# A split-float weight tile on TensorE: the upper part meets both parts of x in one 512-column product

## The chip, the cores and the metric

One core of a Trainium2 chip (trn2) runs the whole program. The metric is the device time of one execution in microseconds; the kernel before was run three times: median 2190.94 us (2187.36 to 2192.04).

## The reference, cut to what matters

Two layers. Each is a token mixer (grouped attention and pooling) followed by a product-key expert mixer; 256 tokens, width 1024, everything in float32. The change is in the expert mixer:

```python
q = (xblk @ w_query).reshape(B, TOKEN_BLOCK, N_PEER_HEADS, 2, SUBKEY_DIM)
s = jnp.einsum('bthpd,hpnd->bthpn', q, sub_keys)
...
u = expert_u[eidx]
h = jnp.einsum('btd,bthkd->bthk', xblk, u)
act = jax.nn.gelu(h, approximate=False) * g
return jnp.einsum('bthk,bthkd->btd', act, expert_v[eidx])
```

The kernel does not gather: it multiplies x with all 16384 rows of `expert_u`, applies Gelu, multiplies by a gate that is zero for every expert a token did not choose, and multiplies with all of `expert_v`.

## The kernel before, in words

**Split operands.** Float32 products are made of three products of the float32r type. Each operand is split in an upper part (`wh`, `xh`: a rounding copy on ACT) and a lower part (`wl`, `xl`: the rest, a subtraction on DVE), and wh·xh + wh·xl + wl·xh is summed in one bank of PSUM. `weights` (L78 to L84) loads a 128x1024 tile by DMA on SP's queue (512 KB, four buffers `raw`), and `split` (L70 to L76) makes `wh` on ACT (L74) and `wl` on DVE (L75), two buffers each.

**A transposed product.** `transposed_product` (L98) takes one weight tile as eight 128x128 blocks and x as eight chunks of 128 rows by 256 tokens. `mm3` (L86 to L96) issues 24 products of 256 columns into half a bank: first 16 with the eight upper blocks, each block twice (against `xh`, then `xl`), and then eight with the lower blocks against `xh`. Every product loads its own stationary block.

**Stages of the expert mixer** (`peer`, L543), once per layer, here called by letters:
- Q: `queries` (L582): 32 tiles of `w_query`, two per bank of tag `mm`, copied out by one ACT instruction (L591); `key_scores` (L593) multiplies a head's queries with its keys; DVE finds the 16 best of each (`top16`, L536).
- U0 and U1: 64 tiles of `expert_u` each (L706 to L720), two tiles per bank of tag `mm`, evicted by one ACT Gelu of 512 columns per pair (L718). Beside U0 runs `routing` on DVE (L622); beside U1 runs `gating` (L676) on DVE and TensorE, for the half of the experts that U0 made.
- V: 128 tiles of `expert_v` (L724 to L741), each 12 products of 512 columns (L738) into four banks of tag `y`; gating of the second half runs beside its first 64 tiles.

**What sets the order.** `Pace` (L234) hands out steps of the side work by rate: `work(1.25)` per tile in U0, `work(1.05)` in U1; `side` hands out the dot products of the modulation (`ada_dot`, L142: one 512 KB load and one DVE instruction of 1024 columns each), 0.3 per tile in U1 of layer 0, none in U of layer 1. The framework places the instructions of each engine in one in-order queue when the program is built; the order in a queue can differ from the order in the text. PSUM has eight banks: two of tag `mm`, two of tag `g` and four of tag `y`; `y` is free in Q and U but for some short products that keep TensorE busy (`keep_warm`, L179).

Of the kernel before, what the change touches and what calls it, by code (L numbers as in the profile page):

```python
# [9 lines left out]
F32 = mybir.dt.float32  # L10
F32R = mybir.dt.float32r
# [3 lines left out]
AF = mybir.ActivationFunctionType  # L15
ALU = mybir.AluOpType
AX = mybir.AxisListType

P = 128
S = 256  # L20
# [29 lines left out]
def encoder_kernel(ctx, tc, x, c, ada_w, small, qkw, w_in1, w_in2, w_attn_o, mix_w, w_pool_o, w_out,  # L50
# [13 lines left out]
    def bank(tag):  # L64
        return psum.tile([P, 512], F32, name=tag, tag=tag, bufs=4 if tag == "y" else 2)
# [12 lines left out]
    def weights(src, shape):  # L78
        raw = rawtile()
        nc.sync.dma_start(raw, src)  # L80
        view = raw if len(shape) == 2 else raw.rearrange("p (a b) -> p a b", b=shape[2])
        if len(shape) == 4:
            view = raw.rearrange("p (a b c) -> p a b c", b=shape[2], c=shape[3])
        return split(view, shape)  # L84

    def mm3(acc, ws, xs, order="wx"):  # L86

        n = len(ws)
        if order == "wx":
            todo = [(k, 0, p) for k in range(n) for p in range(2)] + [(k, 1, 0) for k in range(n)]  # L90
        elif order == "x":
            todo = [(k, w, 0) for k in range(n) for w in range(2)] + [(k, 0, 1) for k in range(n)]
        else:
            todo = [(k, w, p) for k in range(n) for w, p in ((0, 0), (1, 0), (0, 1))]
        for m, (k, w, p) in enumerate(todo):
            PE.matmul(acc, ws[k][w], xs[k][p], start=m == 0, stop=m == 3 * n - 1)  # L96

    def transposed_product(src, xs, acc, order="wx"):  # L98

        wt = weights(src, [P, 8, P])  # L100
        mm3(acc, [(wt[0][:, dc], wt[1][:, dc]) for dc in range(8)],
            [(xs[0][:, dc], xs[1][:, dc]) for dc in range(8)], order)

    zeros = const.tile([P, 512], F16, name="zeros")
    V.memset(zeros, 0.0)
# [113 lines left out]
            return acc  # L219

    def xpair():
        return (xsp.tile([P, 8, S], F32R, name="xh", tag="xh"), xsp.tile([P, 8, S], F32R, name="xl", tag="xl"))

    def modulated(l, which, norm, xs, r, chunks):
        shift = lambda dc: mods[:, l, 24 * which + dc:24 * which + dc + 1]
        xn = lambda dc: norm.space[:, S * dc:S * dc + S]
        for dc in chunks:
            V.scalar_tensor_tensor(xn(dc), xT[:, dc], scaled[:, l, which, dc:dc + 1], r, op0=ALU.mult, op1=ALU.mult)
            A.activation(xs[0][:, dc], xn(dc), AF.Identity, bias=shift(dc))
        for dc in chunks:  # L230
            V.scalar_tensor_tensor(xs[1][:, dc], xn(dc), shift(dc), xs[0][:, dc].bitcast(F32),  # L231
                                   op0=ALU.add, op1=ALU.subtract)

    class Pace:  # L234
# [19 lines left out]
    def mixer(l, arena, parts, norm, side):  # L254
# [5 lines left out]
        probs = [f(52 + 2 * i, 54 + 2 * i).rearrange("p (a s) -> p a s", s=S) for i in range(2)]  # L260
        pTs = [f(56 + 2 * i, 58 + 2 * i).rearrange("p (a s) -> p a s", s=S) for i in range(2)]
        scr = [f(60 + 2 * i, 62 + 2 * i) for i in range(2)]
        pf = lambda a, b: parts[:, a * 256:b * 256].rearrange("p (c t) -> p c t", t=S)
        o = (pf(0, 8), pf(8, 16))
        mixed = (pf(16, 20), pf(20, 24))
        merged = (pf(24, 32), pf(32, 40))

        xs = xpair()

        def column_step(accs, cg, dp):  # L270
            wt = weights(w_in1[l, cg, dp], [P, 2, 512])
            late = l > 0 and cg == 2
            for w, p in ((0, 0), (1, 0), (0, 1)) if late else ((0, 0), (0, 1), (1, 0)):
                for tt in range(NT):
                    for d in range(2):
                        PE.matmul(accs[tt], xs[p][:, 2 * dp + d, tt * P:tt * P + P], wt[w][:, d],  # L276
                                  start=dp + d + w + p == 0, stop=dp == 3 and d == 1 and (p if late else w) == 1)

        def column_end(accs, cg):
# [155 lines left out]
        def values(h):  # L435
            ov = bank("y")[:, :S]
            for sc in range(2):
                v0 = 1280 + h // (NH // NKV) * DH
                PE.matmul(ov, proj[:, sc, v0:v0 + DH], pTs[h % 2][:, sc], start=sc == 0, stop=sc == 1)  # L439
            A.activation(o[0][:, h], ov, AF.Copy)  # L440
            V.tensor_tensor(o[1][:, h], ov, o[0][:, h].bitcast(F32), ALU.subtract)

        def attend(step):
            side(0.9)
# [39 lines left out]
        for g2 in range(2):  # L484
            acc = bank("mm").rearrange("p (a t) -> p a t", t=S)
            for k in range(2):
                g = 2 * g2 + k
                PE.matmul(acc[:, k], mw[:, g * P:g * P + P], mT[:, g], start=True, stop=True)
            for k in range(2):
                g = 2 * g2 + k  # L490
                ps = pscale[:, l, g:g + 1]
                A.activation(mixed[0][:, g], acc[:, k], AF.Copy, scale=ps)
                V.scalar_tensor_tensor(mixed[1][:, g], acc[:, k], ps, mixed[0][:, g].bitcast(F32),
                                       op0=ALU.mult, op1=ALU.subtract)
            if g2 == 0:
                attend(9)
# [4 lines left out]
        for c2 in range(4):  # L501
            pacc = bank("y").rearrange("p (a t) -> p a t", t=S)
            wt = weights(w_pool_o[l, c2], [P, 2, 4, P])
            for k in range(2):
                mm3(pacc[:, k], [(wt[0][:, k, g], wt[1][:, k, g]) for g in range(4)],
                    [(mixed[0][:, g], mixed[1][:, g]) for g in range(4)])
            for k in range(2):
                ct = 2 * c2 + k
                aacc = bank("mm")[:, :S]
                transposed_product(w_attn_o[l, ct], o, aacc)  # L510
                side(0.5)
                ga, gp = gates[:, ct], gates[:, 8 + ct]
                V.tensor_tensor(gp, pacc[:, k], gp, ALU.mult)
                V.tensor_tensor(ga, aacc, ga, ALU.mult)
                V.tensor_tensor(ga, ga, gp, ALU.add)
                A.activation(merged[0][:, ct], ga, AF.Copy)
                V.tensor_tensor(merged[1][:, ct], ga, merged[0][:, ct].bitcast(F32), ALU.subtract)

        norm = Norm(arena[:, 48 * 256:], lean=True)
        for c2 in range(4):  # L520
# [22 lines left out]
    def peer(l, arena, norm, side):  # L543
# [35 lines left out]
        work = Pace()  # L579
        qTs, kts = {}, {}  # L580

        def queries(h, c2):  # L582
            if c2 == 0:
                kts[h] = f(60 + 2 * (h % 2), 62 + 2 * (h % 2))
                nc.sync.dma_start(kts[h], keys[l, h])
                qTs[h] = f(4 * (h % 2), 4 * (h % 2) + 4).rearrange("p (c t) -> p c t", t=S)
            acc = bank("mm").rearrange("p (a t) -> p a t", t=S)
            for k in range(2):
                transposed_product(w_query[l, 4 * h + 2 * c2 + k], xs, acc[:, k], "x" if h + c2 + k == 0 else "wx")
                work(1)  # L590
            A.activation(qTs[h][:, 2 * c2:2 * c2 + 2], acc, AF.Copy)  # L591

        def key_scores(h):  # L593
            sacc = bank("g").rearrange("p (t q n) -> p t q n", t=NT, q=2)
# [110 lines left out]
        for hf in range(2):  # L705
            hb = half.tile([P, 64, S], F32, name="hb", tag="half")  # L706
            hbs.append(hb)
            for i2 in range(32):
                acc = bank("mm").rearrange("p (a t) -> p a t", t=S)
                for k in range(2):  # L710
                    transposed_product(expert_u[l, 64 * hf + 2 * i2 + k], xs, acc[:, k])
                    work(1.25 if hf == 0 else 1.05)
                    if hf:
                        side(0.3)
                if hf == 0 and i2 == 0:
                    key_scores(PH - 1)
                    work.gens.append(late)
                A.activation(hb[:, 2 * i2:2 * i2 + 2], acc, AF.Gelu)  # L718
            work.finish()
            work.gens.append(gating(hb, 64 * hf))  # L720

# [2 lines left out]
        for i in range(128):  # L724
            hb = hbs[i // 64]
            if i == 64:
                work.finish()
            if i % 2 == 0:
                sl = slice(i % 8, i % 8 + 2)
                src = hb[:, i % 64:i % 64 + 2]  # L730
                A.activation(xs[0][:, sl], src, AF.Copy)  # L731
                V.tensor_tensor(xs[1][:, sl], src, xs[0][:, sl].bitcast(F32), ALU.subtract)  # L732
            wt = weights(expert_v[l, i], [P, D])
            todo = [(p, w, tt, d2) for p, w in ((0, 0), (1, 0), (0, 1)) for tt in range(NT) for d2 in range(2)]
            if i == 127:
                todo.sort(key=lambda a: a[2:])
            for p, w, tt, d2 in todo:
                PE.matmul(accs[2 * tt + d2], xs[p][:, i % 8, tt * P:tt * P + P],  # L738
                          wt[w][:, d2 * 512:d2 * 512 + 512], start=i + p + w == 0, stop=i == 127 and w == 1)
            work(1.05)  # L740
            side(0.15 if i < 64 else 0.62)  # L741
# [139 lines left out]
```

## Time and profile before

| what | value |
|---|---|
| median of three runs | 2190.94 us |
| profiled execution, its own time | 2195.78 us |
| span of the profiled execution | 2194.0 us |
| PE busy | 2154.1 us (98%) |
| DVE busy | 1610.6 us (73%) |
| ACT busy | 1015.2 us (46%) |
| mean DMA rate | 191 GB/s |
| mean granted TensorE clock | 0.989 |

The page gives the busy time of each engine, then the chain of work that ended last, followed back from the last instruction, and then the costliest groups of instructions. The durations of products and of vector instructions include a part that overlaps the next one on the same engine, so what one more instruction costs is read from the distance between starts, or from a long chain by its count. Stages are read with the table of stretches, which counts overlapping instructions once.

### The profile page before, as it was taken

To read this page: it belongs to the slowest core of one execution; us is meant where nothing else is said; L and a number is where in the kernel's file an instruction comes from. 1 tells how busy PE (TensorE), PEld (TensorE's weight loads), DVE (VectorE), ACT (ScalarE), POOL (GpSimd) and SP (SyncE) were. 2 spreads that over 40 slices of the span, in tenths; PEclk is the share of its full clock that TensorE was granted. 3 is DMA by queue.
4 is the path that set the end of the run, shared out by engine and by line. 5 is a ranking of instruction groups with operands and counts; after the bars stand their busy time and mean duration, and the time that the engine had idled before them with its cause. 6 is when DMAs were issued, how large, how long until landed. Compare 5 with 4: busy or idle time off the path is not lost.

```text
span 2194.0 us, 38945 instructions
## 1 busy us (share of the span) xinstructions
PE 2154.1 (98%) x15738; PEld 1965.4 (90%) x15738; DVE 1610.6 (73%) x3086; ACT 1015.2 (46%) x1330; POOL 2.1 (0%) x9
## 2 busy tenths in 40 slices
PE   8999999999999999999999999999999999999998
PEld 6889999999999888877789999999999998888887
DVE  6878678846888899867666676796477778886554
ACT  3564445444444444444446644444444444444443
POOL 0000000000000000000000000000000000000000
PEclk8999999999999999999999999999999999999999
DMA  7767454555666666678745345545555555555563
GB/s 267 251 228 234 151 180 158 192 183 196 217 203 213 201 200 198 209 271 275 261 132 196 123 151 186 170 164 193 183 173 164 165 172 173 173 173 184 193 194 100
DMA packets 117093, 419.72 MB, mean 191 GB/s; under 512 B 13008, under 2 KB 14032, under 8 KB 116912
## 3 DMA queue, kind: packets, MB, share of 16 engines
q1 hardware_dynamic: 116784, 416.86, 57.9%
q8 instruction: 123, 2.02, 0.4%
q14 instruction: 58, 0.48, 0.1%
q0 software_dynamic: 128, 0.37, 0.0%
HBM read 416.13 MB, written 1.05 MB: 190 GB/s over the span
## 4 chain that ended last, share of the span: by engine, by line
PE 83%; DMA 7%; DVE 7%; issue 2%; ACT 2%; SPq 0%; DVEq 0%; ACTq 0%
PE mm L96 46%; PE y L738 27%; DMA raw<-in_ada_w_dram 5%; PE g L697 3%; DVE wl L75 3%; PE y L276 2%; PE g L598 1%; PE y L186 1%; PE y L96 1%; ACT wh L74 1%; DMA raw<-in_w_in_dram 1%; PE g L205 1%; DVE raw L143 1%; DMA raw<-in_expert_v_dram 0%; PE y L439 0%
## 5 line engine op out<-in xcount | busy, mean ns | idle before, releaser
L74 ACT ACTIVATE wh<-raw 128x1024 fp32r<-128x1024 f32 x680 | 719.9, 1059 | 1049.0 <-PE mm L96 549.6
L75 DVE TENSOR_TENSOR wl<-raw,wh 128x1024 fp32r<-128x1024 f32 x680 | 829.5, 1221 | 410.9 <-ACT wh L74 409.6
L96 PE MATMUL mm<-xh,wh 128*128 128x256 f32 x2816 | 700.5, 286 | 0.7 <-ACT wh L74 0.7
L96 PE MATMUL mm<-xl,wh 128*128 128x256 f32 x2816 | 691.6, 283 | 0.1
L96 PEld LDWEIGHTS mm<-xl,wh 128*128 128x128 f32 x2816 | 540.2, 192 | 2.4 <-DVE xl L231 2.1
L96 PEld LDWEIGHTS mm<-xh,wh 128*128 128x128 f32 x2816 | 539.7, 192 | 2.4 <-ACT wh L74 0.9
L96 PE MATMUL mm<-xh,wl 128*128 128x256 f32 x2816 | 398.3, 283 | 2.9 <-DVE wl L75 2.8
L96 PEld LDWEIGHTS mm<-xh,wl 128*128 128x128 f32 x2816 | 364.1, 192 | 4.9 <-DVE wl L75 4.6
L738 PE MATMUL y<-wl,xh 128*128 128x512 f32 x1024 | 277.5, 392 | 7.4 <-DVE wl L75 7.2
L738 PE MATMUL y<-wh,xh 128*128 128x512 f32 x1024 | 282.2, 396 | 0.5 <-ACT xh L731 0.5
L738 PE MATMUL y<-wh,xl 128*128 128x512 f32 x1024 | 274.8, 389 | 0.0
L738 PEld LDWEIGHTS y<-wl,xh 128*128 128x128 f32 x1024 | 191.2, 188 | 53.0 <-DVE wl L75 13.8
L738 PEld LDWEIGHTS y<-wh,xl 128*128 128x128 f32 x1024 | 192.4, 188 | 40.6
L738 PEld LDWEIGHTS y<-wh,xh 128*128 128x128 f32 x1024 | 187.9, 189 | 37.2 <-ACT xh L731 0.8
L143 DVE SCALAR_TENSOR_TENSOR raw<-raw,c_b 128x1024 f32<-128x1024 f32 x96 | 116.9, 1222 | 60.5 <-DMA raw<-in_ada_w_dram 60.3
L692 DVE TENSOR_TENSOR pl<-pl,igj 128x512 f16<-128x512 f16 x256 | 107.1, 419 | 2.5
L701 DVE TENSOR_TENSOR hb<-g,hb 128x512 f32<-128x512 f32 x128 | 87.4, 683 | 2.0 <-PE g L697 2.0
L732 DVE TENSOR_TENSOR xl<-hb,xh 128x512 fp32r<-128x512 f32 x128 | 87.1, 683 | 0.7 <-ACT xh L731 0.7
L694 DVE TENSOR_TENSOR ql<-iota_t,igj 128x1024 f16<-128x1024 f16 x128 | 87.4, 683 | 0.0
L697 PEld LDWEIGHTS <-ql 128*128 128x128 f16 x2048 | 68.5, 97 | 19.0 <-issue 16.2
L697 PE MATMUL g<-pl,ql 128*128 128x64 f16 x2048 | 83.7, 193 | 0.0
L731 ACT ACTIVATE xh<-hb 128x512 fp32r<-128x512 f32 x128 | 78.0, 615 | 4.9 <-DVE hb L701 3.8
(182 smaller groups left out, 1463.2 us busy)
## 6 DMA issues: line engine op xcount, KB each, us to landing
raw<-in_expert_u_dram SPq DMA_DIRECT2D x256, 512.0 KB, 3.6
raw<-in_expert_v_dram SPq DMA_DIRECT2D x256, 512.0 KB, 4.0
raw<-in_ada_w_dram SPq DMA_DIRECT2D x96, 512.0 KB, 4.4
raw<-in_w_in_dram SPq DMA_DIRECT2D x64, 512.0 KB, 4.5
raw<-in_w_query_dram SPq DMA_DIRECT2D x64, 512.0 KB, 3.9
raw<-in_w_attn_o_dram SPq DMA_DIRECT2D x16, 512.0 KB, 3.6
raw<-in_w_out_dram SPq DMA_DIRECT2D x16, 512.0 KB, 4.1
raw<-in_w_pool_o_dram SPq DMA_DIRECT2D x8, 512.0 KB, 3.9
```

The lines of the kernel that those rows point to most:

```text
L74: A.activation(h, src, AF.Copy)
L75: V.tensor_tensor(lo, src, h.bitcast(F32), ALU.subtract)
L96: PE.matmul(acc, ws[k][w], xs[k][p], start=m == 0, stop=m == 3 * n - 1)
L143: V.scalar_tensor_tensor(raw, raw, 1.0, c_b, op0=ALU.mult, op1=ALU.mult, accum_out=mods[:, l, m:m + 1])
L276: PE.matmul(accs[tt], xs[p][:, 2 * dp + d, tt * P:tt * P + P], wt[w][:, d], start=dp + d + w + p == 0, stop=dp == 3 and d == 1 and (p if l ...
L692: V.tensor_tensor(pl[:, a], pl[:, 1], row(2 + a, n), ALU.mult)
L694: V.tensor_tensor(ql, count(0, NK), row(1, NK), ALU.is_equal)
L697: PE.matmul(gp[:, t], ql[:, t // 2, :, t % 2], pl[:, a, t // 2, :, t % 2], start=a == 0, stop=a == 1)
L701: V.tensor_tensor(hv, gp.rearrange("p t i -> p i t"), hv, ALU.mult)
L731: A.activation(xs[0][:, sl], src, AF.Copy)
L732: V.tensor_tensor(xs[1][:, sl], src, xs[0][:, sl].bitcast(F32), ALU.subtract)
L738: PE.matmul(accs[2 * tt + d2], xs[p][:, i % 8, tt * P:tt * P + P], wt[w][:, d2 * 512:d2 * 512 + 512], start=i + p + w == 0, stop=i == 127 ...
```

## The change

For Q, U0 and U1, `halved_product` takes the place of `transposed_product`. The two parts of x lie beside each other in one tile (`x2`, chunk by part by token), so that an upper weight block meets `xh` and `xl` in one product of 512 columns; the two results land in the two halves of a bank. The lower blocks then add wl·xh to the first half. A tile has a bank of its own, of tag `y` (the last four tiles of U1 take tag `mm`). `merge` brings the halves together: ACT copies the second half into SBUF, DVE adds the first. Gelu then runs in place in SBUF, per pair as before. The first query tile of each layer keeps 24 products of 256 columns. Every other user of the pair `xs[0]`, `xs[1]` (and of `o`, `mixed`, `merged` in the mixer) is rewritten to the joint layout with the same instructions.

```diff
+    def halved_product(src, xs, acc, order="wx"):
+
+        wh, wl = weights(src, [P, 8, P])
+        if order == "x":
...
+        for k in range(8):
+            PE.matmul(acc, wh[:, k], xs[:, k], start=k == 0, stop=False, skip_group_check=True)
+        for k in range(8):
+            PE.matmul(acc[:, 0], wl[:, k], xs[:, k, 0], start=False, stop=k == 7, skip_group_check=True)
...
-        return (xsp.tile([P, 8, S], F32R, name="xh", tag="xh"), xsp.tile([P, 8, S], F32R, name="xl", tag="xl"))
+        return xsp.tile([P, 8, 2, S], F32R, name="x2", tag="x2")
...
+        def halves(tag):
+            return bank(tag).rearrange("p (a t) -> p a t", t=S)
+
+        def merge(dst, acc):
+            A.activation(dst, acc[:, 1], AF.Copy)
+            V.tensor_tensor(dst, acc[:, 0], dst, ALU.add)
...
-            acc = bank("mm").rearrange("p (a t) -> p a t", t=S)
             for k in range(2):
-                transposed_product(w_query[l, 4 * h + 2 * c2 + k], xs, acc[:, k], "x" if h + c2 + k == 0 else "wx")
+                acc = halves("y")
+                halved_product(w_query[l, 4 * h + 2 * c2 + k], xs, acc, "x" if h + c2 + k == 0 else "wx")
                 work(1)
-            A.activation(qTs[h][:, 2 * c2:2 * c2 + 2], acc, AF.Copy)
+                merge(qTs[h][:, 2 * c2 + k], acc)
...
             for i2 in range(32):
-                acc = bank("mm").rearrange("p (a t) -> p a t", t=S)
                 for k in range(2):
-                    transposed_product(expert_u[l, 64 * hf + 2 * i2 + k], xs, acc[:, k])
+                    acc = halves("mm" if hf and i2 > 29 else "y")
+                    halved_product(expert_u[l, 64 * hf + 2 * i2 + k], xs, acc)
+                    merge(hb[:, 2 * i2 + k], acc)
                     work(1.25 if hf == 0 else 1.05)
...
-                A.activation(hb[:, 2 * i2:2 * i2 + 2], acc, AF.Gelu)
+                two = hb[:, 2 * i2:2 * i2 + 2]
+                A.activation(two, two, AF.Gelu)
...
-                A.activation(xs[0][:, sl], src, AF.Copy)
-                V.tensor_tensor(xs[1][:, sl], src, xs[0][:, sl].bitcast(F32), ALU.subtract)
+                A.activation(xs[:, sl, 0], src, AF.Copy)
+                V.tensor_tensor(xs[:, sl, 1], src, xs[:, sl, 0].bitcast(F32), ALU.subtract)
```

## Rows read from the trace of the kernel before

**Rows 1.** The page, part 1: busy time, share of the span, instructions.

```profile
PE 2154.1 (98%) x15738; PEld 1965.4 (90%) x15738; DVE 1610.6 (73%) x3086; ACT 1015.2 (46%) x1330; POOL 2.1 (0%) x9
```

**Rows 2.** The page, part 4: the chain that ended last, by line.

```profile
PE mm L96 46%; PE y L738 27%; DMA raw<-in_ada_w_dram 5%; PE g L697 3%; DVE wl L75 3%; PE y L276 2%; PE g L598 1%; PE y L186 1%; PE y L96 1%; ACT wh L74 1%; DMA raw<-in_w_in_dram 1%; PE g L205 1%; DVE raw L143 1%; DMA raw<-in_expert_v_dram 0%; PE y L439 0%
```

**Rows 3.** The chain in order of time, longest pieces: start us, us, what.

```profile
383.73 139.46 PE mm L96 x1160
...
1991.13 182.34 PE y L738 x804
```

**Rows 4.** Stretches U1, U1, U0, Q: length, PE, PEld, DVE, ACT, POOL busy, PE clock, DMA.

```profile
532.95:722.70 189.75, 189.75 (x1933) 188.42 (x1933) 160.34 (x251) 77.28 (x90) 0.00 (x0) 1.00 0.66 212
1609.63:1799.40 189.77, 189.77 (x1933) 188.44 (x1932) 142.90 (x218) 77.27 (x90) 0.00 (x0) 1.00 0.51 167
345.50:523.80 178.30, 177.24 (x1473) 176.51 (x1471) 122.26 (x308) 83.28 (x96) 0.00 (x0) 1.00 0.55 180
...
235.87:345.50 109.63, 109.63 (x923) 109.63 (x924) 74.46 (x258) 49.76 (x59) 0.00 (x0) 1.00 0.52 173
```

**Rows 5.** Groups by form: line engine op, shapes, count | busy, mean ns | idle before.

```profile
L75 DVE TENSOR_TENSOR wl<-raw,wh 128x1024 fp32r<-128x1024 f32 x680 | 829.5, 1221 | 410.9 <-ACT wh L74 409.6
L74 ACT ACTIVATE wh<-raw 128x1024 fp32r<-128x1024 f32 x680 | 719.9, 1059 | 1049.0 <-PE mm L96 549.6 <-PE y L738 331.1 <-DMA raw<-in_expert_v_dram 51.5
...
L701 DVE TENSOR_TENSOR hb<-g,hb 128x512 f32<-128x512 f32 x128 | 87.4, 683 | 2.0 <-PE g L697 2.0
L732 DVE TENSOR_TENSOR xl<-hb,xh 128x512 fp32r<-128x512 f32 x128 | 87.1, 683 | 0.7 <-ACT xh L731 0.7
...
L731 ACT ACTIVATE xh<-hb 128x512 fp32r<-128x512 f32 x128 | 78.0, 615 | 4.9 <-DVE hb L701 3.8 <-PE y L738 1.1
L718 ACT ACTIVATE hb<-mm 128x512 f32<-128x512 f32 x128 | 75.9, 593 | 0.2
...
L514 DVE TENSOR_TENSOR arena<-mm,arena 128x256 f32<-128x256 f32 x16 | 6.8, 422 | 9.1 <-PE mm L96 9.1
...
L440 ACT ACTIVATE parts<-y 128x256 fp32r<-128x256 f32 x16 | 6.2, 386 | 1.9 <-PE y L439 1.9
```

**Rows 6.** DVE in order of time in U1 of layer 0: start us, us, instruction.

```profile
600.49 0.68 DVE L701 TENSOR_TENSOR hb<-g,hb 128x512 f32<-128x512 f32 x1
601.09 0.42 DVE L690 TENSOR_TENSOR pl<-iota_t,igj 128x512 f16<-128x512 f16 x1
601.42 0.68 DVE L694 TENSOR_TENSOR ql<-iota_t,igj 128x1024 f16<-128x1024 f16 x1
602.02 0.42 DVE L692 TENSOR_TENSOR pl<-pl,igj 128x512 f16<-128x512 f16 x1
602.36 1.22 DVE L143 SCALAR_TENSOR_TENSOR raw<-raw,c_b 128x1024 f32<-128x1024 f32 x1
```

**Rows 7.** ACT in order of time in U1 of layer 0.

```profile
601.70 1.06 ACT L74 ACTIVATE wh<-raw 128x1024 fp32r<-128x1024 f32 x1 [2.39 <-PE mm L96]
602.66 0.59 ACT L718 ACTIVATE hb<-mm 128x512 f32<-128x512 f32 x1
604.58 1.06 ACT L74 ACTIVATE wh<-raw 128x1024 fp32r<-128x1024 f32 x1 [1.32 <-PE mm L96]
```

**Rows 8.** Waits in U1 of layer 0, 532 to 722 us: total, times, longest.

```profile
DVE wl L75 <- ACT wh L74: 21.8, 21, 1.6
DVE raw L143 <- DMA raw<-in_ada_w_dram: 6.4, 7, 1.1
```

**Rows 9.** The chain in order of time at the start of U0, layer 0.

```profile
357.00 1.61 DVE arena L616 x9
...
382.54 1.14 DVE wl L75
383.73 8.30 PE mm L96 x67
```

**Rows 10.** The chain where U1 of layer 0 hands over to V.

```profile
729.68 0.63 ACT xh L731
```

More of the change, by code (lines that the diff above doesn't have):

```diff
@@ L95, in mm3 @@
         for m, (k, w, p) in enumerate(todo):
-            PE.matmul(acc, ws[k][w], xs[k][p], start=m == 0, stop=m == 3 * n - 1)
+            PE.matmul(acc, ws[k][w], xs[k][:, p], start=m == 0, stop=m == 3 * n - 1)
     def transposed_product(src, xs, acc, order="wx"):
@@ L101, in transposed_product @@
         mm3(acc, [(wt[0][:, dc], wt[1][:, dc]) for dc in range(8)],
-            [(xs[0][:, dc], xs[1][:, dc]) for dc in range(8)], order)
+            [xs[:, dc] for dc in range(8)], order)
+    def halved_product(src, xs, acc, order="wx"):
+        wh, wl = weights(src, [P, 8, P])
+        if order == "x":
+            for k in range(8):
+                for w in (wh, wl):
+                    PE.matmul(acc[:, 0], w[:, k], xs[:, k, 0], start=k == 0 and w is wh, stop=k == 7 and w is wl)
+            for k in range(8):
+                PE.matmul(acc[:, 1], wh[:, k], xs[:, k, 1], start=k == 0, stop=k == 7)
+            return
+        for k in range(8):
+            PE.matmul(acc, wh[:, k], xs[:, k], start=k == 0, stop=False, skip_group_check=True)
+        for k in range(8):
+            PE.matmul(acc[:, 0], wl[:, k], xs[:, k, 0], start=False, stop=k == 7, skip_group_check=True)
     zeros = const.tile([P, 512], F16, name="zeros")
@@ L228, in modulated @@
             V.scalar_tensor_tensor(xn(dc), xT[:, dc], scaled[:, l, which, dc:dc + 1], r, op0=ALU.mult, op1=ALU.mult)
-            A.activation(xs[0][:, dc], xn(dc), AF.Identity, bias=shift(dc))
+            A.activation(xs[:, dc, 0], xn(dc), AF.Identity, bias=shift(dc))
         for dc in chunks:
-            V.scalar_tensor_tensor(xs[1][:, dc], xn(dc), shift(dc), xs[0][:, dc].bitcast(F32),
+            V.scalar_tensor_tensor(xs[:, dc, 1], xn(dc), shift(dc), xs[:, dc, 0].bitcast(F32),
                                    op0=ALU.add, op1=ALU.subtract)
@@ L262, in mixer @@
         scr = [f(60 + 2 * i, 62 + 2 * i) for i in range(2)]
[L263 to L266, printed above, removed]
+        pf = lambda a, b: parts[:, a * 256:b * 256].rearrange("p (c w t) -> p c w t", w=2, t=S)
+        o, mixed, merged = pf(0, 16), pf(16, 24), pf(24, 40)
         xs = xpair()
@@ L275, in column_step @@
                     for d in range(2):
-                        PE.matmul(accs[tt], xs[p][:, 2 * dp + d, tt * P:tt * P + P], wt[w][:, d],
+                        PE.matmul(accs[tt], xs[:, 2 * dp + d, p, tt * P:tt * P + P], wt[w][:, d],
                                   start=dp + d + w + p == 0, stop=dp == 3 and d == 1 and (p if late else w) == 1)
@@ L439, in values @@
                 PE.matmul(ov, proj[:, sc, v0:v0 + DH], pTs[h % 2][:, sc], start=sc == 0, stop=sc == 1)
-            A.activation(o[0][:, h], ov, AF.Copy)
-            V.tensor_tensor(o[1][:, h], ov, o[0][:, h].bitcast(F32), ALU.subtract)
+            A.activation(o[:, h, 0], ov, AF.Copy)
+            V.tensor_tensor(o[:, h, 1], ov, o[:, h, 0].bitcast(F32), ALU.subtract)
         def attend(step):
@@ L491, in mixer @@
                 ps = pscale[:, l, g:g + 1]
-                A.activation(mixed[0][:, g], acc[:, k], AF.Copy, scale=ps)
-                V.scalar_tensor_tensor(mixed[1][:, g], acc[:, k], ps, mixed[0][:, g].bitcast(F32),
+                A.activation(mixed[:, g, 0], acc[:, k], AF.Copy, scale=ps)
+                V.scalar_tensor_tensor(mixed[:, g, 1], acc[:, k], ps, mixed[:, g, 0].bitcast(F32),
                                        op0=ALU.mult, op1=ALU.subtract)
@@ L505, in mixer @@
                 mm3(pacc[:, k], [(wt[0][:, k, g], wt[1][:, k, g]) for g in range(4)],
-                    [(mixed[0][:, g], mixed[1][:, g]) for g in range(4)])
+                    [mixed[:, g] for g in range(4)])
             for k in range(2):
@@ L515, in mixer @@
                 V.tensor_tensor(ga, ga, gp, ALU.add)
-                A.activation(merged[0][:, ct], ga, AF.Copy)
-                V.tensor_tensor(merged[1][:, ct], ga, merged[0][:, ct].bitcast(F32), ALU.subtract)
+                A.activation(merged[:, ct, 0], ga, AF.Copy)
+                V.tensor_tensor(merged[:, ct, 1], ga, merged[:, ct, 0].bitcast(F32), ALU.subtract)
         norm = Norm(arena[:, 48 * 256:], lean=True)
@@ L737, in peer @@
             for p, w, tt, d2 in todo:
-                PE.matmul(accs[2 * tt + d2], xs[p][:, i % 8, tt * P:tt * P + P],
+                PE.matmul(accs[2 * tt + d2], xs[:, i % 8, p, tt * P:tt * P + P],
                           wt[w][:, d2 * 512:d2 * 512 + 512], start=i + p + w == 0, stop=i == 127 and w == 1)
```

## The prediction

> **What bounds the kernel now.** I began with the busy times: PE at 98%, DVE at 73%, ACT at 46% [rows 1]. A busy PE alone says little, so the chain came next: 46% of the span is the products of L96, 27% those of L738, and only 3% the lower-part subtraction of DVE [rows 2]. The changed stages are therefore bound by the distance from one product to the next, and the chain by time gives it: 1160 products of 256 columns in 139.46 us, 120.2 ns each; 804 products of 512 columns, in V, in 182.34 us, 226.8 ns each [rows 3]. The busy durations of products are longer than this and overlap, so I don't use them. Last I read the stretches, for what lies beside: in 189.75 us of U1 DVE is busy 160.34 us in layer 0, 142.90 in layer 1; in U0 122.26 of 178.30; in Q 74.46 of 109.63; ACT is below half everywhere [rows 4].
>
> **Products.** A tile has 24 products of 256 columns now: 24 x 120.2 = 2885 ns. Afterwards it has 8 of 512 and 8 of 256: 8 x 226.8 + 8 x 120.2 = 2776 ns. It gains 109 ns, because two columns' worth of work is the same and only what a product costs beyond its columns is saved: 2 x 120.2 - 226.8 = 13.6 ns, eight times. Changed tiles: 2 layers x (32 + 128) less the first of each layer, 318. **Gain: 318 x 109 = 34.7 us.** The 226.8 ns are from V, where 512 columns of moving data also meet a new stationary block each time, so I take them. The other end is two products' price, 240.4 ns and no gain; a product cheaper than V's is excluded, since V's run back to back at the full clock.
>
> The two distances in [rows 3] leave 13.6 ns per product that don't depend on the columns. The Trainium skill ("TensorE: Matmul & The Clock Gate", section "Wait — 56ns, not 53.3ns?") puts this fixed part at about 2.5 ns; by it, 318 x 8 x 2.5 ns, an estimate of 6 us, would be all the gain. The trace does not agree with the page, and the measured distances decide.
>
> **Merges: DVE.** New: one addition of 128x256 per tile, one input in PSUM. L514 is the same operation, 422 ns [rows 5]. In a full queue it costs less: L690, 0.42 us long, is followed after 0.33 us, L694 (0.68) after 0.60 [rows 6], some 0.08 us of overlap. So 0.34 us per tile, at most 0.42. What that does differs by stage:
> - Q: 33 tiles, 74.46 + 11.2 = 85.7 us of DVE against 109.63 - 3.6 = 106 of PE. Covered; at nothing.
> - U1, layer 1: 60 tiles, 142.90 + 20.4 = 163.3 against 189.77 - 6.5 = 183.2. Covered; if that cover went, each tile would cost its 0.34 us.
> - U1, layer 0: 160.34 + 20.4 = 180.7, and DVE also waits 6.4 us for loads of the modulation [rows 8], which it will wait again: 187.1 against 183.2. DVE becomes the bound by 3.9 us in 60 tiles; I take **4 us lost**. Ends: none lost, if the loads land earlier relative to a later DVE; or, with the full 0.42 us and the 21.8 us that DVE waits for ACT [rows 8] kept too, 213.7 against 183.2, 30 us lost. I stay near the low end because waits for ACT come from DVE being early, and a late DVE doesn't have them.
> - U0: in sum covered (122.26 + 61 x 0.34 = 143 against 171.6), but not evenly. From 357.00 to 383.73 us the chain runs on DVE's routing and subtractions [rows 9]. That stretch holds some ten tiles: ten additions (3.4 us) are put into it, and PE's gain of 1.1 us there can't be had. I take 2.5 us per layer, **5 us lost** (ends: none, as PE may be ahead by its two buffers; 4.5 per layer).
>
> **Merges: ACT.** New: a copy of 128x256 from PSUM per tile, 386 ns as L440; Gelu reads SBUF in place of PSUM, 615 ns as L731 against 593 [rows 5]. In U1 77.28 + 60 x 0.386 + 30 x 0.022 = 101 of 183 us; in Q L591's copies go. Covered by ACT's idle time, which goes mostly to waiting for PE (549.6 us before L74) [rows 5].
>
> **The waits that the merges add.** DVE's addition waits for ACT's copy, the copy for the tile's products (I reckon with its last product, both halves being in one bank; no row shows whether it could be sooner), and Gelu for the addition of the pair's second tile. On ACT the next `wh` stands behind Gelu; on DVE the next `wl`, gating and the modulation stand behind the addition; PE waits for both. Today the split stands ahead of Gelu in ACT's queue, though later in the text: L74 at 601.70, L718 at 602.66, L74 at 604.58 [rows 7]. If this order is kept, copy, addition and Gelu take about 0.39 + 0.42 + 0.62 = 1.4 us after a tile's end. The split two tiles on is already running then; the one after it can start when the upper blocks of the next tile are through (8 x 226.8 = 1.8 us) and is needed 2 x 2776 ns after the tile's end. So it may start as late as 5.55 - 1.06 = 4.5 us after that end, and copy, addition and Gelu may together lose 4.5 - 1.4 = 3.1 us before PE notices. At nothing outside the saturated stretches, which are counted above.
>
> **Layout, banks, hand-over.** Writes into the joint tile have a gap between chunks; L701 reads a scattered operand at 683 ns, as L732 a plain one [rows 5], so nothing, neither way. Tag `y` gives four banks with one tile each instead of two with two; a bank has about 8 us to be emptied. DMAs and SP's queue are as they were; a tile every 2.78 us asks for 4% more rate. Where U1 ends, ACT's `xh` is on the chain [rows 10]; the last merge and a later gating may add 0.5 us per layer: **1 us lost** (0 to 2).
>
> **Sum.** -34.7 + 4 + 5 + 1 = -24.7 us. On the profiled execution, 2195.8, that gives 2171; the median of the runs is 4.8 us lower, and on it I forecast 2190.9 - 24.7 = **2166 us**.
>
> **Rivals.**
> 1. *DVE hides all of it.* The losses don't appear: 2190.9 - 34.7 = 2156. For it: the routing stretch cost PE little before, PE being 177.24 of 178.30 us busy in U0 [rows 4]. Against: the sum of U1, layer 0.
> 2. *ACT waits for DVE, slower.* Place: Gelu in U0 and U1. ACT waited for PE alone there; now Gelu sits behind the addition, and that may sit behind a gating batch (some 2.2 us of L701, L690, L694 and two of L692), a `wl` (1.15) and a dot product (1.15), with its load. Then `wh` is late, so `wl` too, and PE waits. From that queue, 4.5 us in sum, less the 3.1 us of slack, 1.4 us could be lost in a bad pair. It decides from 34.7 / 128 pairs = 0.27 us per pair; at 0.5 us per pair in all 128 pairs the time is 2190.9 - 34.7 + 64 = 2220. For it: DVE already at 84% in U1 of layer 0 and in-order queues. Against: an order like that of [rows 7], and DVE at 78% in U1 of layer 1 and below 70% in U0 [rows 4].
> 3. *The wide product saves nothing here*: its distance is 240 ns. Then PE leaves DVE room as before, and only U0 and the hand-over cost: up to 2197, most likely 2191. Against: [rows 3]. By the page's 2.5 ns above, it would be 2185 before losses, on this side.
>
> **Chances.** A measurement of this kernel tells 0.2%, 4.4 us, from no change, so 2186.5 to 2195.3 is the same. The forecast 0.58; every loss covered 0.09; a mix in which DVE eats 10 to 25 us more than I took (2176 to 2191) 0.13, of which 0.08 is still faster; rival 2 0.15, as the order of the changed queues can't be read from this trace; rival 3 0.05, of which 0.04 is the same. Faster 0.58 + 0.09 + 0.08 = 0.75, same 0.05 + 0.04 = 0.09, slower 0.15 + 0.01 = 0.16. The range goes from rival 1 less the scatter of the runs, 2154, into the beginning of rival 2, 2196, and leaves out its far part.
>
> **What would show it.** Right: in V 227 ns as now, and in Q and U chains with 16 products per tile at about 2.78 us a tile; PE's waits for `wl` only early in U0 and in U1 of layer 0; some 134 us of additions on DVE and 123 us of copies on ACT. Wrong: products of 512 columns at 240 ns; Gelu waiting for DVE pair after pair with `wh` late behind it; a tile distance above 2.9 us in U1 of layer 1, where DVE has room.

## The result and the profile after

The changed kernel takes 2158.11 us (median of four runs, 2156.65 to 2158.76), the kernel before 2191.49 us in the same comparison: ratio 0.9849, 95% interval 0.9836 to 0.9863, so 33.4 us less. The profiled execution has a span of 2157.0 us. The forecast was 2166 us, a gain of 24.7 us.

The page after is to be set beside [rows 1, 2, 5]. PE's products fall from 15738 to 13194, and DVE and ACT gain the instructions of the merges:

```profile
PE 2121.9 (98%) x13194; PEld 1827.3 (85%) x13194; DVE 1711.3 (79%) x3406; ACT 1095.6 (51%) x1618; POOL 2.1 (0%) x9
...
PE y L760 27%; PE y L115 26%; PE y L117 13%; PE mm L96 5%; DMA raw<-in_ada_w_dram 4%; PE g L717 3%; PE y L289 3%; DVE wl L75 2%; PE g L618 1%; PE y L201 1%; PE y L96 1%; DMA raw<-in_w_in_dram 1%; DVE raw L158 1%; ACT wh L74 1%; PE g L220 1%
...
L740 ACT ACTIVATE hb<-hb 128x512 f32<-128x512 f32 x128 | 80.7, 630 | 126.3 <-DVE hb L600 126.2
...
L600 DVE TENSOR_TENSOR hb<-y,hb 128x256 f32<-128x256 f32 x248 | 103.4, 417 | 2.7 <-ACT hb L599 2.4
L599 ACT ACTIVATE hb<-y 128x256 f32<-128x256 f32 x248 | 90.7, 366 | 0.0
```

L115 is the wide product, L117 the narrow one, L599 and L600 the merge, L740 Gelu, L760 V's product. The chain is still products: 26% and 13% in place of 46% for L96. Gelu waits 126.2 us in all for the addition, so the wait that the prediction feared is there; whether PE feels it, the chain shows. The chain in order of time, in U0 of layer 0 (start us, us, what), to be set beside [rows 3]:

```profile
335.35 1.85 PE y L115 x8
337.20 0.95 PE y L117 x8
338.15 1.84 PE y L115 x8
339.99 0.95 PE y L117 x8
340.94 1.84 PE y L115 x8
```

A tile takes 2.794 us (ten tiles on, at 363.29, the same pattern starts again: 27.94 us). The forecast was 2.776. For the kernel before, the prediction had 2.885 from the mean of a long chain; where nothing disturbs them, its tiles start every 2.880 us in the trace. The narrow products keep their 0.12 us; the wide ones take 1.84 / 8 = 0.230 us on average, 3 ns more than V's 226.8.

The stretches of U1 (layer 0, 30 pairs), Q and U0 in the columns of [rows 4]:

```profile
515.56:700.40 184.84, 184.84 (x1465) 163.28 (x1463) 179.28 (x314) 96.97 (x150) 0.00 (x0) 1.00 0.66 219
242.70:333.56 90.86, 90.86 (x563) 81.40 (x562) 75.81 (x280) 41.94 (x64) 0.00 (x0) 1.00 0.53 181
335.35:507.17 171.82, 171.63 (x983) 150.35 (x983) 141.24 (x368) 101.01 (x157) 0.00 (x0) 1.00 0.54 186
```

In U1 of layer 0 DVE is busy 179.28 of 184.84 us, 97%, and PE has no gap: DVE at 97% costs nothing here. The waits of that stage (515 to 700 us) say why, beside [rows 8]:

```profile
ACT hb L740 <- DVE hb L600: 26.9, 28, 2.1
...
DVE wl L75 <- ACT wh L74: 2.7, 7, 0.9
DVE raw L158 <- DMA raw<-in_ada_w_dram: 1.3, 2, 1.0
```

DVE's wait for the modulation's loads went from 6.4 to 1.3 us and its wait for ACT from 21.8 to 2.7: a later DVE finds its inputs there. Gelu's longest wait is 2.1 us in this stage, below the 3.1 us that the prediction allowed.

**Where the time went.** The changed stages run from Q's first product to V's first. In the chain of the changed kernel these two are, for both layers:

```profile
224.58 2.74 PE y L110 x14
...
708.13 1.18 PE y L760 x4
...
1284.83 2.74 PE y L110 x14
...
1768.41 1.18 PE y L760 x4
```

So 483.6 us in each layer. The same in the kernel before:

```profile
231.38 2.89 PE mm L96 x19
...
730.36 11.19 PE y L738 x48
...
1307.36 3.59 PE mm L96 x19
...
1807.04 11.21 PE y L738 x48
```

That is 499.0 and 499.7 us, 31.5 us more in all. The other 2 us of the 33.4 lie outside the changed stages.

### The profile page after: what moved, and what is told of

Read it like the earlier page. It is cut to its first block, busy times and chain, and to the rows that moved or that the text cites. A ratio compares the mean times of both kernels' runs of the same rounds, so it can differ in the third digit from the quotient of the medians.

```text
span 2157.0 us, 34508 instructions
## 1 busy us (share of the span) xinstructions
PE 2121.9 (98%) x13194; PEld 1827.3 (85%) x13194; DVE 1711.3 (79%) x3406; ACT 1095.6 (51%) x1618; POOL 2.1 (0%) x9
## 4 chain that ended last, share of the span: by engine, by line
PE 86%; DMA 6%; DVE 5%; issue 2%; ACT 2%; SPq 0%; DVEq 0%; ACTq 0%
PE y L760 27%; PE y L115 26%; PE y L117 13%; PE mm L96 5%; DMA raw<-in_ada_w_dram 4%; PE g L717 3%; PE y L289 3%; DVE wl L75 2%; PE g L618 1%; PE y L201 1%; PE y L96 1%; DMA raw<-in_w_in_dram 1%; DVE raw L158 1%; ACT wh L74 1%; PE g L220 1%
## 5 line engine op out<-in xcount | busy, mean ns | idle before, releaser
L75 DVE TENSOR_TENSOR wl<-raw,wh 128x1024 fp32r<-128x1024 f32 x680 | 829.3, 1220 | 290.9 <-ACT wh L74 289.2
L115 PE MATMUL y<-x,wh 128*128 128x512 f32 x2480 | 629.7, 395 | 0.0
L760 PE MATMUL y<-wh,x 128*128 128x512 f32 x2048 | 514.2, 392 | 1.4 <-ACT wh L74 0.9
L115 PEld LDWEIGHTS y<-x,wh 128*128 128x128 f32 x2480 | 445.3, 189 | 80.2 <-ACT wh L74 0.4
L760 PEld LDWEIGHTS y<-wh,x 128*128 128x128 f32 x2048 | 379.3, 188 | 79.4 <-ACT wh L74 2.6
L117 PEld LDWEIGHTS y<-x,wl 128*128 128x128 f32 x2480 | 337.8, 190 | 26.3 <-DVE wl L75 2.5
L117 PE MATMUL y<-x,wl 128*128 128x256 f32 x2480 | 346.1, 282 | 0.4 <-DVE wl L75 0.4
L760 PE MATMUL y<-wl,x 128*128 128x512 f32 x1024 | 276.6, 391 | 7.4 <-DVE wl L75 7.2
L760 PEld LDWEIGHTS y<-wl,x 128*128 128x128 f32 x1024 | 190.9, 188 | 52.4 <-DVE wl L75 13.4
L740 ACT ACTIVATE hb<-hb 128x512 f32<-128x512 f32 x128 | 80.7, 630 | 126.3 <-DVE hb L600 126.2
L600 DVE TENSOR_TENSOR hb<-y,hb 128x256 f32<-128x256 f32 x248 | 103.4, 417 | 2.7 <-ACT hb L599 2.4
L599 ACT ACTIVATE hb<-y 128x256 f32<-128x256 f32 x248 | 90.7, 366 | 0.0
L96 PE MATMUL mm<-parts,wh 128*128 128x256 f32 x512 | 69.3, 284 | 0.7 <-DVE parts L530 0.7
```

What stands on the lines that cost most here:

```text
L75: V.tensor_tensor(lo, src, h.bitcast(F32), ALU.subtract)
L96: PE.matmul(acc, ws[k][w], xs[k][:, p], start=m == 0, stop=m == 3 * n - 1)
L115: PE.matmul(acc, wh[:, k], xs[:, k], start=k == 0, stop=False, skip_group_check=True)
L117: PE.matmul(acc[:, 0], wl[:, k], xs[:, k, 0], start=False, stop=k == 7, skip_group_check=True)
L599: A.activation(dst, acc[:, 1], AF.Copy)
L600: V.tensor_tensor(dst, acc[:, 0], dst, ALU.add)
```

## The experiments

Medians, the ratio to the kernel before on the same chip (95% interval), and the changed stages by the trace, Q's first product to V's first, layer 0 and layer 1:

| run | median us | ratio | layer 0, us | layer 1, us |
|---|---|---|---|---|
| changed kernel | 2158.1 | 0.9849 (0.9836 to 0.9863) | 483.6 | 483.6 |
| changed kernel again | 2157.3 | 0.9829 (0.9813 to 0.9844) | 483.6 | 483.6 |
| before again | 2191.4 | 0.9997 (0.9982 to 1.0012) | 499.7 | 499.7 |
| narrow products, merges kept | 2192.2 | 1.0007 (0.9996 to 1.0018) | 498.3 | 498.3 |
| before, own banks | 2190.1 | 0.9993 (0.9984 to 1.0003) | 498.4 | 498.4 |
| no addition | 2160.7 | 0.9857 (0.9838 to 0.9876) | 485.0 | 485.0 |
| two additions | 2188.5 | 0.9996 (0.9981 to 1.0010) | 512.4 | 483.0 |
| two banks | 2163.2 | 0.9872 (0.9854 to 0.9890) | 486.4 | 486.4 |
| gates too | 2156.0 | 0.9830 (0.9816 to 0.9843) | 483.6 | 483.6 |
| alternating | 2184.5 | 0.9966 (0.9952 to 0.9980) | 500.8 | 494.5 |

Two theories were set against each other. The first: the distance between products is the gain, and the merges cost nothing as long as DVE's work fits beside PE. The rival: the gain comes from own banks or another queue order, or the additions do cost PE time that something else pays back.

**The wide product alone undone.**

```diff
         for k in range(8):
-            PE.matmul(acc, wh[:, k], xs[:, k], start=k == 0, stop=False, skip_group_check=True)
+            for p in range(2):
+                PE.matmul(acc[:, p], wh[:, k], xs[:, k, p], start=k + p == 0, stop=False, skip_group_check=True)
```

> The changed kernel with the wide product taken back alone: 24 products of 256 columns per tile, in the same two halves, own banks and merges kept. If the distance between products is the whole gain, each of 2544 pairs costs 240.4 ns again in place of the 229.9 ns read from the changed kernel's chain: 2544 x 10.5 ns = 27 us, so about 2185 us (2182 to 2189). If the gain came from banks and queue order, it stays within 8 us of 2158.

Measured 2192.2 us: all of the gain is gone. The stages take 996.6 us together against 967.1, 29.5 us more; the chain of U0 in this run shows tiles of 1.92 + 0.96 us:

```profile
402.04 1.92 PE y L116 x16
403.96 0.96 PE y L118 x8
404.92 1.92 PE y L116 x16
```

That is 11.6 ns for each of 2544 pairs, near the 10.5 expected. Undisturbed tiles are 2.88 us apart here (402.04 to 404.92) and 2.793 with the wide product, 87 ns less, or 10.9 ns a pair. The time missed its range by 3 us, and 34.1 - 29.5 = 4.6 us of the difference lie outside the changed stages. Against the kernel before (998.7 us in its first profile, 999.4 in its second) the merges, own banks and halves of this run are 2 to 3 us ahead in the stages, and the time is the same. The first theory holds.

**Own banks alone, in the kernel before.**

```diff
-                acc = bank("mm").rearrange("p (a t) -> p a t", t=S)
                 for k in range(2):
-                    transposed_product(expert_u[l, 64 * hf + 2 * i2 + k], xs, acc[:, k])
+                    acc = bank("mm" if hf and i2 > 29 else "y")[:, :S]
+                    transposed_product(expert_u[l, 64 * hf + 2 * i2 + k], xs, acc)
+                    A.activation(hb[:, 2 * i2 + k], acc, AF.Gelu)
...
-                A.activation(hb[:, 2 * i2:2 * i2 + 2], acc, AF.Gelu)
```

> The kernel before with one bank of tag y per tile and an eviction of 256 columns per tile (Copy or Gelu on ACT); products as before, no addition on DVE. If the distance between products is the whole gain, only the start of Q improves (the second tile fills the gaps of the first, about 1 us per layer): 2187 to 2191 us. If own banks are what paid, it goes below 2180.

The copies of the queries are changed in the same way. Measured 2190.1 us, as the first theory had it. Its stages are 498.4 us in each layer, 0.6 and 1.3 us shorter than in the first profile of the kernel before and 1.3 in both than in the second; own banks pay about that and no more.

**The addition left out.**

```diff
-            A.activation(dst, acc[:, 1], AF.Copy)
-            V.tensor_tensor(dst, acc[:, 0], dst, ALU.add)
+            A.activation(dst, acc[:, 0], AF.Copy)
```

> The changed kernel without DVE's addition (the half wh.xl is left out of the result; ACT copies the first half). If DVE's 97% in U1 of layer 0 and its stretch in U0 cost nothing but the stall of about 1 us at the start of each U0, 2154 to 2158 us. If the saturated DVE costs as much as the prediction charged (9 us), 2147 to 2150 us.

Measured 2160.7 us, and 485.0 us per layer, 1.4 us more than with the addition. Taking some 133 us of additions (318 x 0.417 us) from DVE gains nothing. The 1.4 us lie at the start of U0, beside DVE's routing. Added up over the tiles there, what goes beyond the undisturbed 2.793 us is 0.8 us in the changed kernel, 2.2 us without the addition, and nothing in the run with two additions below; the kernel before, beyond its 2.880, has 2.0. So the stall there doesn't grow with the additions; what sets it isn't shown. Both ranges were missed on the upper side, the first by 3 us.

**One addition more.**

```diff
             A.activation(dst, acc[:, 1], AF.Copy)
+            spare = tmp.tile([P, S], F32, name="spare", tag="spare")
+            V.tensor_tensor(spare, acc[:, 0], dst, ALU.subtract)
             V.tensor_tensor(dst, acc[:, 0], dst, ALU.add)
```

> The changed kernel with one more DVE instruction of 128x256 per tile, ahead of the addition, into a spare tile. If DVE is hidden until its queue is full, U1 of layer 0 goes from 179.3 busy of 184.8 us to 199.7 and is bound by DVE (+15 us), the start of U0 loses 2 us per layer more, the rest is covered: 2174 to 2182 us. If Gelu waiting for the addition decides, every U stage suffers: 64 tiles x 4 stages x 0.34 us = 87 us at most, above 2195. If PE has more slack than the sums say, below 2165.

Measured 2188.5 us: 30 us lost, where 16 to 24 were expected. It all falls in U1 of layer 0: the first gating product is at 511.0 us, V's first at 733.1, 222.1 us in place of 192.7 (515.4 to 708.1). Layer 1, where DVE has no modulation to do, pays nothing (483.0 us), though DVE is busy 186.4 of 192.8 us in its U1, again 97%. The two stretches, from the first gating product to V's first, in layers 0 and 1 of this run:

```profile
511.00:733.10 222.10, 200.25 (x1507) 166.34 (x1505) 205.44 (x384) 104.92 (x159) 0.00 (x0) 1.00 0.58 187
...
1598.40:1791.20 192.80, 192.26 (x1523) 169.82 (x1521) 186.43 (x351) 101.48 (x159) 0.00 (x0) 1.00 0.52 172
```

In layer 0 DVE is demanded for 205 us in a stage that PE would end after 193. But the stage takes 222, 17 us longer than DVE is busy. The waits of this stage name what came on top:

```profile
ACT wh L74 <- DVE wl L75: 46.3, 25, 3.4
ACT wh L74 <- DMA raw<-in_expert_u_dram: 37.1, 26, 3.1
PEld y L117 <- DVE wl L75: 15.6, 14, 1.8
PEld y L115 <- ACT wh L74: 15.6, 16, 1.5
ACT hb L599 <- PE y L117: 14.8, 21, 1.4
```

ACT's upper part waited for loads of `expert_u` 26 times; in the changed kernel's waits of that stage no such row stands. The chain of this run shows the circle:

```profile
567.46 1.15 DVE wl L75
...
568.66 5.30 DMA raw<-in_expert_u_dram
...
574.06 1.06 ACT wh L74
...
575.43 0.42 DVE spare L601
```

The split's subtraction on DVE (L75) is the last reader of a raw tile. When it comes late, the load into that buffer starts late (568.66), and its 5.3 us stand on the chain instead of behind work. The loads of `expert_u` themselves are hardly longer than in this stage of the changed kernel (median 4.2 us from issue to landing against 4.1). The copy of the half, L599, waits for the narrow products L117 (14.8 us), that is for a tile's last product: the answer to what the prediction had left open. The Trainium skill ("PSUM — Partial Sum Buffer", section "Terms") says that two engines must not be in one bank and quadrant at a time. The order in the trace fits this, in that the copy of a finished half stands behind the products of the other; no run tells whether it must.

**The loads taken out, DVE's work kept.** A first attempt put a DVE reduction of 1024 columns, of a tile that was there from the start, in place of each of the modulation's dot products in U1 of layer 0:

> The kernel with two additions per tile, in which the modulation's dot products of U1 of layer 0 (one 512 KB load and one DVE instruction each) become DVE reductions of the same width without a load; the dot products themselves move into V and lengthen it, so only the stage is read: from the first gating product to V's first product, 222 us with two additions, 193 us with one. If the late DVE loses time through the load buffers that it and the dot products hold, the stage falls to about 205 us, its DVE time. If a full DVE alone makes the loss, it stays at 215 to 222 us.

Of the loads it tells nothing: the reductions waited for nothing, and the trace has all of them before 157 us, none in the stage. It is one more case of 97%, though: with two additions and no dot products DVE was busy 186.26 us there, as in the changed kernel (186.48), and the stage took 192.7. The second attempt ties each reduction to finished tiles of the same stage:

```diff
-                    if hf:
-                        side(0.3)
+                    if hf and l == 0:
+                        idle_due[0] += 0.3
+                        if idle_due[0] >= 1 and 2 * i2 + k >= 8:
+                            idle_due[0] -= 1
+                            j = 2 * i2 + k - 8
+                            V.tensor_reduce(idle, hb[:, j:j + 4].rearrange("p a b -> p (a b)"), AX.X, ALU.max)
```

> As the run with the reductions in place of the modulation's dot products, but each reduction reads four finished tiles of Gelu (1024 columns, written five to eight tiles before), so that it can't be moved ahead of U1: two additions per tile, 19 reductions of about 1.2 us, no loads for them in U1 of layer 0. DVE's demand is then that of the run with two additions, 205 us busy. If the loss there (222 in place of 193 us from the first gating product to V's first) comes from load buffers held by a late DVE, the stage takes 203 to 208 us; if a full DVE makes all of it, 215 to 222 us.

The stretch of U1 in layer 0, and two of its waits:

```profile
515.20:726.80 211.60, 198.44 (x1506) 168.87 (x1504) 205.96 (x365) 106.10 (x159) 0.00 (x0) 0.99 0.48 156
```

```profile
ACT wh L74 <- DVE wl L75: 73.7, 41, 3.6
...
PE y L117 <- DVE wl L75: 10.4, 10, 1.9
```

DVE is as busy as in the run with two additions (205.96 against 205.44 us), and the stage takes 211.6 in place of 222.1: between the two ranges. So 10.5 us of the 29.4 lost there are lost only with the modulation's loads beside a late DVE; ACT's 37.1 us of waits for loads are gone. How much of this is buffers held and how much is fewer loads isn't separated: the loads left in the stage also land sooner (median 3.4 us against 4.2). The other 18.9 us stay without them. DVE's work is 13.3 us more than PE's 192.7, and 5.6 us of the stage DVE is idle; part of it may be TensorE's clock, which was granted at the lower level, 1.2 GHz, from 626.5 to 629.9 us, after PE had stood 1.9 us waiting for DVE. The whole runs of the two attempts (2179.6 and 2197.4 us, one each) say nothing, since the dot products moved into V.

**Two banks in place of four.**

```diff
-                    acc = halves("mm" if hf and i2 > 29 else "y")
+                    acc = halves("mm")
```

Q's tiles are changed in the same way.

> The changed kernel with all tiles of Q, U0 and U1 in the two banks of tag mm in place of the four of y. A bank must then be emptied in one tile's time (2.8 us) instead of three. If copy and addition follow a tile's end closely, nothing changes (2156 to 2160 us). If the additions stand behind gating, subtraction and dot product for up to 3.5 us, as Gelu's waits of up to 2.7 us for the addition suggest, PE waits for banks in U0's start and in U1: 2165 to 2190 us.

Measured 2163.2 us, between the two ranges, against 2157.3 of the changed kernel on the same chip (ratios 0.9872 and 0.9829, intervals apart). The stages take 2.8 us more in each layer, 2.5 of them at the start of U0, where the stall grows from 0.8 to 3.3 us. Bank depth is worth that much.

**The gate tiles too.**

```diff
-                transposed_product(w_in2[l, c0 + k], xs, acc[:, k])
+                acc = halves("mm")
+                halved_product(w_in2[l, c0 + k], xs, acc)
+                merge(gates[:, c0 + k], acc)
...
-            A.activation(gates[:, c0:c0 + 2], acc, AF.Copy)
```

> The changed kernel with the 16 gate tiles of each layer's mixer (w_in2) done in the same way, in tag mm. 32 tiles at 0.09 us are 2.9 us if that stage is bound by the distance of products: 2155 us (2153 to 2157). If it is bound by loads or by DVE's side work there, no change, 2157 to 2160 us, or more with the additions on DVE.

Measured 2156.0 against 2157.3 us of the changed kernel on the same chip, with ratios of 0.9830 and 0.9829: no difference that can be told, though the time lies in the first range. It is faster than the kernel before, but not shown faster than the changed one. Of the 15 distances between gate tiles in layer 0, four are the undisturbed 2.8 us and ten are 3.0 to 6.9 us: most of that stage isn't bound by products.

**Both kernels again.**

> The changed kernel unaltered, for a second profile and more times. If the 6.6 us that its first profile gained ahead of Q in layer 0, where nothing was changed, are the draw of single executions, Q of layer 0 starts anywhere between 220 and 232 us and the median stays at 2158 (2156 to 2160).

> The kernel before, unaltered, for a second profile. The changed stages (Q's first product to V's first) should take 499 us in layer 0 and 500 in layer 1 again, as they took 483.6 four times in the two profiles of the changed kernel; Q of layer 0 may start anywhere between 220 and 232 us if that is a draw, near 231 again if the kernels differ there.

Second profile of the changed kernel, Q's first product and, ahead of it, the last short products that wait for the norm:

```profile
224.79 1.30 PE y L201 x6
226.09 2.74 PE y L110 x14
```

Second profile of the kernel before, Q's and V's first products:

```profile
232.34 3.59 PE mm L96 x19
...
732.03 3.03 PE y L738 x12
...
1305.79 3.59 PE mm L96 x19
...
1805.48 4.64 PE y L738 x19
```

The stages repeat within 0.8 us. Q of layer 0 starts at 224.6 and 226.1 us with the change, at 231.4 and 232.3 without. But it starts at 231.7 with narrow products and merges and at 220.7 with two additions, whose instructions up to Q are the changed kernel's in the same order. So the start of Q scatters by up to 11 us between executions of the same work; what makes it do so is not settled. It stands outside the changed stages, and of the 33.4 us by the medians no more than some 2 us lie there (33.4 - 31.5).

**Where the 3 ns of a wide product come from.**

```diff
         for k in range(8):
             PE.matmul(acc, wh[:, k], xs[:, k], start=k == 0, stop=False, skip_group_check=True)
-        for k in range(8):
             PE.matmul(acc[:, 0], wl[:, k], xs[:, k, 0], start=False, stop=k == 7, skip_group_check=True)
```

> The changed kernel with wide and narrow products alternating block by block (16 per tile as before). In the changed kernel eight wide products take 1.84 us, 230 ns each, where V's take 227. If the 3 ns come from two wide products with different blocks in a row, a tile falls from 2.794 to about 2.776 us and the time by 5 us, to 2152 us. If wl is needed too early (at a tile's start instead of 1.8 us into it), PE waits for DVE in U0's start and in U1 of layer 0: 2160 to 2180 us.

Measured 2184.5 us. Many tiles keep the distances of the changed kernel or worse, 0.23 or 0.24 and 0.12 us:

```profile
399.93 0.23 PE y L115
400.17 0.12 PE y L116
400.28 0.24 PE y L115
400.52 0.12 PE y L116
```

But a part of the tiles, where no wait falls into them, is faster, such as this one with its 16 products:

```profile
1548.38 0.39 PE L115 MATMUL y<-x,wh 128*128 128x512 f32 x1
...
1551.15 0.39 PE L115 MATMUL y<-x,wh 128*128 128x512 f32 x1
```

In U0 of layer 1, 15 of 63 tile distances are 2.773 to 2.776 us, the forecast's 2.776: a wide and a narrow product together take 347 ns there, 226.8 + 120.2. Elsewhere in this run a pair takes 350 and every third 360. In the changed kernel, too, the 3 ns are no price of each wide product. From start to start (medians over its tiles) the first five wide products take 228 to 236 ns, the last three 227 as in V, and the first narrow one 113 in place of 120. So the wide product can have V's distance in these stages; which order of the queue gives it, and why, stays open. The rest went as expected of a `wl` needed 1.8 us earlier, only by more: from Q to the end of U1 of layer 0 the lower blocks' weight loads wait 33 times for DVE's `wl` and the products 11 times, 19.3 us together. The order of the change, all upper blocks first, is what gives DVE its time.

## Why the prediction was right

**Products (forecast 34.7 us).** The mechanism is shown: undoing the wide product alone takes everything back. The size was too large. An undisturbed tile gained 87 ns (2.880 to 2.793 us), not 109: 318 x 87 ns = 27.7 us, 7.0 less. This is the term that was mis-sized against the change. Most of it is the wide product, which took 230 ns on average here and not V's 226.8; the rest, 5 ns a tile, is that the 120.2 ns were the mean of a chain that held a few longer distances. The distance at V was the nearest row, and the alternating run shows that it can be had here too; the changed kernel's order doesn't get it in the first wide products of a tile. By the Trainium skill ("TensorE: Matmul & The Clock Gate", section "Wait — 56ns, not 53.3ns?"), with 2.5 ns of fixed cost per product, an estimate of 6 us would have been all; the runs don't agree with it for these products (87 / 8 = 10.9 ns saved per pair), and decide.

**DVE in U1 of layer 0 (forecast 4 us lost).** Wrong: nothing was lost. The sum put DVE's 6.4 us wait for loads beside its 180.7 us as if it would stay; 1.3 us of it stayed. The busy time itself was well sized (179.28 for 180.7), so the price of an addition, 0.34 us, held nearly (18.9 us for 60). The prediction argued that waits for ACT vanish when DVE is late, and should have said the same of the loads.

**U0 (forecast 5 us lost).** Wrong, in the sign too. DVE's stretch is on the chain again, from 380.06 to 385.04 us, but the stage was stalled before as well, by 2.0 us, and now by 0.8. Its 64 tiles with the last score products fell by 6.7 us (key scores at 343.73 to gating at 532.46, against 333.56 to 515.56), more than 64 x 87 ns = 5.6. The prediction put ten additions into a DVE stretch as if the rest of it stayed as it was; the runs with no addition (2.2 us of stall) and two (none) show that the stall doesn't follow their number.

**Hand-over (forecast 1 us lost), start of Q (at nothing).** The first lost nothing visible. The start of Q gained instead: the first tile waits for chunks of x, and a second tile in a bank of its own fills these gaps. The run with own banks alone shows 0.6 and 1.3 us in the two layers against the first profile of the kernel before. So the stages add up: 27.7 from products, 2.4 from U0's stall, 1.9 from the start of Q, less 0.5 because a tile in U1 gained 83 ns and not 87, makes 31.5, as measured. That the time came within 8 us of the forecast is in part luck: the products gave 7 us less than forecast, while losses of 10 us did not come and small gains of 4 us were not foreseen.

**ACT and Gelu (at nothing), rival 2 (ACT waits for DVE).** Gelu did wait for the addition, 126 us in all, up to 2.7 us; PE did not notice, as the slack of 3.1 us had it. Rival 2 was right about the wait and wrong about the price. Its condition came true only with a second addition, and there the price came by another way: raw tiles held by a late subtraction, so late loads. **Rival 1** (all covered, 2156 us) came nearest to the time, and its reason, that DVE hides the merges, is right; its size, 34.7 us, was not what the products gave. **Rival 3** is out: no undisturbed wide product takes 240 ns. One reading in the rivals was off: DVE was at 75% in U1 of layer 1 (142.90 of 189.77 us), not 78%; nothing hangs on it.

## What to carry to other kernels

Where products follow each other at a distance of columns plus a fixed part (13.6 ns here), joining two that share a stationary block saves most of the fixed part (10.9 ns a pair here), and the merge that this needs is free as long as its engines stay below full. Judge "full" by busy time without the waits that lateness removes: at 97% DVE cost nothing in three stages, and in the two runs where its work went 13 us beyond PE's, the stage lost 18.9 and 29.4 us. The engine that reads a load buffer last sets when the next load starts, so a full engine there turns hidden loads into waits.

## What the runs showed of the hardware that was not expected

The same 512-column product in float32r, at a granted clock of 1.00, took 228 to 236 ns as one of the first five after narrow products and 227 ns as one of the last three, and 227 ns in V, where x is stationary and the weights move; strictly alternating with narrow products it came to 347 ns for the two, or to 350 and 360, tile by tile. And a DVE that was busy 97% of 184.84 us left PE without a gap, while a demand of 205 us in a 193 us stage cost 18.9 us without loads beside it, and 29.4 us with them.
